# Bias products first, table transfers on SyncE, half of a down product held at the change of phase

## The chip, the cores and the metric

The kernel runs on one core of a Trainium2 chip. The metric is the device time of one launch in microseconds (us); a smaller time is better. The kernel is written in a Python layer in which tiles and instructions are traced in program order. A planner then fixes the order of the instructions on every engine when the program is built, from a simulated timeline (`schedule_with_timeline_sim=True`): of the instructions that are ready in the simulation, the one that stands earlier in the program goes first. On the chip every engine works through its list in that fixed order.

## The reference, cut to what matters

One decoder layer is run for 1024 prompt tokens and 64 sample tokens, in float32, with model width 1024 and inner width 2816:

```python
x = x + 0.5 * swiglu(rmsnorm(x, norm_ffn1), ffn1_w_up, ffn1_w_down)   # FFN 1
h = rmsnorm(x, norm_mix);  q, k, v, u, g_a, g_b = split(h @ w_in)
A = dilated_attention(q, k, v, relative_bias)     # three head groups
B = multiscale_pool(u)
x = x + (sigmoid(g_a) * (A @ w_a) + sigmoid(g_b) * (B @ w_p)) @ w_out
x = x + 0.5 * swiglu(rmsnorm(x, norm_ffn2), ffn2_w_up, ffn2_w_down)   # FFN 2

def swiglu(x, w_up, w_down):
    gate, up = split(x @ w_up)
    return (silu(gate) * up) @ w_down
```

The relative bias is a table of 32 rows (one for each bucket of distance) by 12 heads. It is looked up by distance and added to the logits of the attention. The outputs also hold new key and value caches, which for the most part are copies of the old ones.

## The kernel before, in words

**Products.** Each float32 operand is split into a high and a low part (`split`, L216: ScalarE writes the high part, VectorE or GpSimd subtracts it), and each product is three matmuls (`mm3`, L266): high by high, high by low, low by high.

**The FFN (`ffn`, L411, called once for each FFN).** The product with `w_up` is made in blocks of two by two with seven products instead of eight, in the manner of Strassen and Winograd. The tokens are cut into two phases: phase 0 has 512 tokens (two halves of 256), phase 1 has 576 (two halves of 288). A phase has 11 columns `j` (`jj` counts 22 over both phases), and a column has two units, `kind` 0 for the gate and `kind` 1 for the up part. A unit loads two tiles `ur` of 512 KB (`load_unit`, L418, four buffers, so two units) and makes seven left sides from them (`prepare`, L426: four additions on GpSimd at L435 to L440, and seven splits). The left sides are made `LEAD` = 5 products ahead of the product that uses them (`product`, L449). The first product of a unit is copied out by ScalarE at L526.

The seven right sides of a phase are made once, from the tokens' rows, by `right_sides` (L373): VectorE scales by the row statistics (L382), GpSimd and VectorE subtract (L389), ScalarE and VectorE split (L394, L395). They all lie in `h_hi` and `h_lo`, where the right sides of the phase before also lie.

`result` (L512) turns the products of the two units into the hidden column: VectorE adds (L520), VectorE multiplies by the gate (L522), ScalarE makes the high part `hh` (L217) and GpSimd the low part `hl` (L218). The product with `w_down` of a column (`down`, L471) follows one column later. `down_some` (L486) places two of its eight output blocks `d` at each of four places between the products of the next column. `down_weights` (L460) loads and splits the two halves of a column's `w_down` into tiles `wh` and `wl`, of which there are three sets. At the end of phase 0 all eight blocks of the last column follow together (L543), and then the right sides of phase 1 are made; at the end of phase 1 the last column is done for the tokens in two chunks (L546), and `hook` starts the norm of what follows (L645 in FFN 1) or emits the output transposes (FFN 2).

**The start.** SyncE loads nine tiles of rows (`xn`, L583). TensorE transposes them into `xt` (L596), and ScalarE and VectorE evict (L602, L604). The statistics of the first four tiles are made along the way, and with them the right sides of phase 0 (L617). Then `biases` (L562) makes four products of the one-hot table `oh` with the bias table `tb` (L570), copies them to `fr` (three buffers, L572) and sends them to DRAM as `f_scr` (L573, a GpSimd transfer). The pools of these tiles (`bp` and `ip`) are closed at L619, and `ffn` opens its own pool in the same room.

**The tables.** From `f_scr` 47 transfers between L626 and L639, all issued by GpSimd, spread the bias into tables in DRAM for the attention: 44 pieces of `b_scr` (the smallest 1 KB) and three tables `f_rep` of 896 KB. The first reader of any of them runs after FFN 1.

**Order between jobs.** The `Interleaver` (L74) keeps a clock of its own, in planned microseconds, which `mm3` and `down` advance; a job spawned on it runs its next step when its planned time has come. `some_copies` (L210) places copies of the old caches behind the last weight load on SyncE.

The functions that the change touches:

Of the kernel before, what the change touches and what calls it, by code (L numbers as in the profile page):

```python
# [119 lines left out]
def body(ctx, tc, x_prompt, x_sample, c128, c512, c2048, state_pool, rel_bias_table,  # L120
# [290 lines left out]
    def ffn(xt, gi, w_up, w_down, hook):  # L411


        fctx = ExitStack()
        fp = fctx.enter_context(tc.tile_pool(name="fp", bufs=1, side="right"))
        raws, s1s, left, downs = {}, {}, {}, {}

        def load_unit(n):  # L418
            if n < 44:
                c0 = (n % 2) * DFF + (n % 22 // 2) * 256  # L420
                raws[n] = [fp.tile([P, 4, 256], F32, tag="ur", name="ur", bufs=4) for _ in range(2)]
                for i in range(2):
                    load(raws[n][i], w_up[i * 512:(i + 1) * 512, c0:c0 + 256].rearrange(
                        "(k p) n -> p k n", p=P))

        def prepare(i):  # L426

            n, q = divmod(i, 7)
            if n >= 44:
                return  # L430
            a11, a21 = [raws[n][0][:, :, f * P:(f + 1) * P] for f in range(2)]
            a12, a22 = [raws[n][1][:, :, f * P:(f + 1) * P] for f in range(2)]
            if q == 0:
                s1s[n] = fp.tile([P, 4, P], F32, tag="s1", name="s1", bufs=1)
                G.tensor_tensor(out=s1s[n], in0=a21, in1=a22, op=ALU.add)  # L435
                G.tensor_tensor(out=a21, in0=a11, in1=a21, op=ALU.subtract)
            src = (a11, a12, a11, s1s[n], a21, a22, a12)[q]
            if q == 2:
                G.tensor_tensor(out=a11, in0=s1s[n], in1=a11, op=ALU.subtract)  # L439
                G.tensor_tensor(out=a12, in0=a12, in1=a11, op=ALU.subtract)  # L440
            left[i] = [fp.tile([P, 4, P], F32R, tag=x, name=x, bufs=LEAD + 1) for x in ("sh", "sl")]
            split(*left[i], src)
            if q == 6:
                del raws[n]
                load_unit(n + 2)

        made = [0]

        def product(i, p):  # L449
            while made[0] <= i + LEAD:  # L450
                prepare(made[0])
                made[0] += 1
            lh, ll = left.pop(i)
            bank = psa()[:, :PHASES[p][1]]
            mm3(bank, [(lh[:, k, :], ll[:, k, :], *operand(p, i % 7, k)) for k in range(4)],
                0.36)
            il.advance(0.36)
            return bank

        def down_weights(jj, f):  # L460
            r = wp.tile([P, D], F32, tag="wr", name="wr", bufs=3)
            load(r, w_down[(2 * (jj % 11) + f) * P:(2 * (jj % 11) + f + 1) * P, :])
            w = [wp.tile([P, D], F32R, tag=x, name=x) for x in ("wh", "wl")]
            for a in range(2):
                sl = slice(a * 512, (a + 1) * 512)
                split(w[0][:, sl], w[1][:, sl], r[:, sl], G)
            downs.setdefault(jj, []).append(w)
            if f == 0:
                some_copies(1)

        def down(jj, hid, d, c0, n):  # L471
            hh, hl = hid
            t0 = PHASES[jj // 11][0]
            o = psb()[:, :n]
            sl = slice(d * P, (d + 1) * P)
            mm3(o, [(downs[jj][f][0][:, sl], downs[jj][f][1][:, sl],
                     hh[:, f, c0 - t0:c0 - t0 + n], hl[:, f, c0 - t0:c0 - t0 + n]) for f in range(2)])
            xd = xt[:, d, c0:c0 + n]
            V.scalar_tensor_tensor(out=xd, in0=o, scalar=0.5, in1=xd, op0=ALU.mult, op1=ALU.add)  # L479
            il.advance(0.0026 * n)  # L480

        def chunks(p):
            t0, m = PHASES[p]
            return [(0, 512)] if p == 0 else [(t0, m), (t0 + m, m)]

        def down_some(jj, hid, ds):  # L486
            if hid is not None:
                for d in ds:
                    for c0, n in chunks(jj // 11):
                        down(jj, hid, d, c0, n)  # L490
                    hook(jj, None, d)

        load_unit(0)
        load_unit(1)
        prev = None
        for jj in range(22):
            p, j = divmod(jj, 11)
            t0, m = PHASES[p]
            if j == 0:
                if p:  # L500
                    right_sides(xt, gi, p, [over_rows(diagonal(st, m)) for st in sts])
                prev = None
            if jj == 1:
                sts = [stat() for _ in range(2)]
                for h in range(2):
                    il.spawn(sumsq(xt, PHASES[1][0] + h * PHASES[1][1], PHASES[1][1], sts[h]), 8 * h)
            hid = [fp.tile([P, 2, 576], F32R, tag=x, name=x, bufs=2) for x in ("hh", "hl")]
            sil = {}
            for kind in range(2):
                n = 2 * jj + kind  # L510

                def result(r, s, bank, part, kept):  # L512

                    if kind == 0:
                        t = sil[r, s] = fp.tile([P, 288], F32, tag="si", name="si", bufs=4)[:, :m]
                        V.tensor_tensor(out=t, in0=part, in1=bank, op=ALU.add)  # L516
                        S.activation(t, t, AF.Silu)
                    else:
                        c = tmp()[:, :m] if kept else part
                        V.tensor_tensor(out=c, in0=part, in1=bank, op=ALU.add)  # L520
                        t = sil[r, s]
                        V.tensor_tensor(out=c, in0=c, in1=t, op=ALU.mult)  # L522
                        split(hid[0][:, r, s * m:(s + 1) * m], hid[1][:, r, s * m:(s + 1) * m], c, G)

                a, b = tmp()[:, :m], tmp()[:, :m]
                S.activation(a, product(7 * n, p), AF.Copy)  # L526
                result(0, 0, product(7 * n + 1, p), a, True)
                V.tensor_tensor(out=a, in0=a, in1=product(7 * n + 2, p), op=ALU.add)
                V.tensor_tensor(out=b, in0=a, in1=product(7 * n + 3, p), op=ALU.add)
                down_some(jj - 1, prev, (4 * kind, 4 * kind + 1))  # L530
                o = product(7 * n + 4, p)
                result(1, 1, o, b, True)
                V.tensor_tensor(out=a, in0=a, in1=o, op=ALU.add)
                if kind:
                    down_weights(jj, 0)
                down_some(jj - 1, prev, (4 * kind + 2, 4 * kind + 3))
                if kind:
                    down_weights(jj, 1)
                result(1, 0, product(7 * n + 5, p), a, False)
                result(0, 1, product(7 * n + 6, p), b, False)  # L540
            prev = hid
            if j == 10 and p == 0:
                down_some(jj, prev, range(KD))  # L543
            elif j == 10:
                hook(jj, -1, 0)
                for i, (c0, n) in enumerate(chunks(1)):  # L546
                    for d in range(KD):
                        down(jj, prev, d, c0, n)
                        hook(jj, i, d)
        fctx.close()  # L550
# [29 lines left out]
    for t in range(ntile):  # L580
        rows = P if t < 8 else NS
        xn = ip.tile([P, D], F32, tag="xn", name="xn", bufs=7)
        load(xn[:rows], xp[t * P:(t + 1) * P, :] if t < 8 else xs)  # L583
        xns.append(xn)
    first = []
    for tiles in ((0, 1), (2, 3), (4, 5, 6, 7, 8)):
        for t in tiles:
# [27 lines left out]
        first.append(over_rows(dg))  # L615
        if tiles[0] == 2:
            right_sides(xt, 0, 0, first)  # L617
    biases()
    ictx.close()  # L619
    bctx.close()  # L620

    def fbias(g, off, ap):
        return bass.AP(tensor=f_scr.tensor, offset=f_scr.offset + g * 4 * BL + off, ap=ap)


    for g in range(3):  # L626
        G.dma_start(out=b_scr[g][:, :, P:], in_=neg.unsqueeze(1).to_broadcast([NS, 4, NS]))
        if g == 2:
            G.dma_start(out=b_scr[g][:, :, :P], in_=fbias(g, 127, [[0, NS], [BL, 4], [1, P]]))
        else:  # L630
            for q in range(Q):
                G.dma_start(out=b_scr[g][q::Q, :, :P],
                            in_=fbias(g, 127 - q // DIL[g], [[0, B], [BL, 4], [1, P]]))
        for b in range(B):
            G.dma_start(out=b_scr[g][b * Q:(b + 1) * Q, :, P + b * Q:P + (b + 1) * Q],
                        in_=fbias(g, 384, [[Q, Q], [BL, 4], [1, Q]]))

    for g in (0, 1, 3):
        G.dma_start(out=f_rep[g], in_=fbias(g, 0, [[BL, 4], [0, P], [1, BL]]))  # L639

    def spill(c):
        c0, n = CH[c]
# [794 lines left out]
```

## Time and profile before

| | |
|---|---|
| three runs | 2517.49, 2519.24, 2520.58 us; median 2519.24 us |
| profiled execution | 2517.62 us, span 2515.9 us from first to last instruction |
| TensorE matmul busy | 2363.3 us (94%) |
| VectorE, GpSimd, ScalarE busy | 1817.6 (72%), 1136.1 (45%), 975.9 us (39%) |
| mean granted TensorE clock | 0.953 of full speed |

The rows further down are of one profiled execution. PE is the matmul side of TensorE, DVE is VectorE, ACT is ScalarE, POOL is GpSimd, SP is SyncE, and a trailing q (SPq) is an engine's sequencer, which issues transfers. "L271 psa<-h_hi,sh" names the line, the written tile and the tiles read; lines 271 to 273 are the three matmuls of `mm3`. "[4.58 <-ACT hh L217]" behind an instruction says how long its engine was idle before it and what ended that. A granted clock of 1.00 is 2.4 GHz and 0.50 is 1.2 GHz.

### The profile page before, as it was taken

The numbers are of one execution on the slowest core, as the hardware profiler recorded it, in microseconds if no ns is written. First come the engines' busy times: TensorE is split into PE (matmuls) and PEld (weight loads), VectorE is DVE, ScalarE is ACT, GpSimd is POOL, SyncE is SP. The second block draws the span as 40 slices with busy tenths as digits, with TensorE's granted clock in tenths as the row PEclk, the third lists the DMA queues.
The fourth block names the chain that finished last, engine by engine and source line by source line (L and its number), as shares of the span: only waits on it lengthen the run. The fifth ranks groups of instructions, "written<-read, shape, count | busy, mean of one in ns | idle before, by whom it ended". The sixth has DMA issues, their size and how long they took to land. (4 is left out here: it accounts for less than half of the span.)

```text
span 2515.9 us, 42145 instructions
## 1 busy us (share of the span) xinstructions
PE 2363.3 (94%) x15894; PEld 2235.3 (89%) x15894; DVE 1817.6 (72%) x3246; ACT 975.9 (39%) x2130; POOL 1136.1 (45%) x1060
## 2 busy tenths in 40 slices
PE   4499999799999989999999999997999998999999
PEld 2489998699999989999999889996899987999998
DVE  5498888788888863366677424629988888788886
ACT  4244444343443433344333222214444443444442
POOL 6656666556555431201011110105666665566554
PEclk7799999799999989999899999997999997999999
DMA  6223343333324122457565773622244432333251
GB/s 189 78 80 109 109 134 134 124 101 118 118 101 134 50 68 83 152 163 233 181 193 177 244 233 118 217 76 75 88 140 140 152 138 68 126 127 127 92 201 38
DMA packets 208314, 328.72 MB, mean 131 GB/s; under 512 B 16272, under 2 KB 171600, under 8 KB 207328
## 3 DMA queue, kind: packets, MB, share of 16 engines
q1 hardware_dynamic: 194096, 293.48, 35.6%
q0 software_dynamic: 14016, 32.56, 3.7%
q8 instruction: 125, 2.05, 0.3%
q14 instruction: 77, 0.63, 0.1%
HBM read 297.10 MB, written 76.32 MB: 148 GB/s over the span
## 5 line engine op out<-in xcount | busy, mean ns | idle before, releaser
L271 PE MATMUL psa<-h_hi,sh 128*128 128x256 f32 (+1 forms) x2464 | 724.9, 295 | 62.1 <-ACT sh L217 51.0
L272 PE MATMUL psa<-h_lo,sh 128*128 128x256 f32 (+1 forms) x2464 | 727.9, 295 | 18.7 <-DVE h_lo L395 18.3
L273 PE MATMUL psa<-h_hi,sl 128*128 128x256 f32 (+1 forms) x2464 | 723.1, 294 | 0.0
L218 DVE TENSOR_TENSOR sl<-ur,sh 128x512 fp32r<-128x512 f32 x528 | 589.5, 1123 | 109.9 <-ACT sh L217 99.9
L271 PEld LDWEIGHTS psa<-h_hi,sh 128*128 128x128 f32 x2464 | 474.2, 193 | 77.4 <-ACT sh L217 52.8
L272 PEld LDWEIGHTS psa<-h_lo,sh 128*128 128x128 f32 x2464 | 474.7, 193 | 33.6 <-DVE h_lo L395 29.3
L273 PEld LDWEIGHTS psa<-h_hi,sl 128*128 128x128 f32 x2464 | 475.6, 193 | 0.5 <-DVE sl L218 0.5
L217 ACT ACTIVATE sh<-ur 128x512 fp32r<-128x512 f32 x528 | 330.3, 627 | 370.3 <-POOL ur L439 187.2
L272 PE MATMUL psa<-h_lo,wh 128*128 128x360 f32 (+1 forms) x1104 | 374.7, 339 | 5.5 <-DVE h_lo L364 5.5
L271 PE MATMUL psa<-h_hi,wh 128*128 128x360 f32 (+1 forms) x1104 | 376.6, 342 | 3.4 <-ACT h_hi L363 3.4
L273 PE MATMUL psa<-h_hi,wl 128*128 128x360 f32 (+1 forms) x1104 | 370.9, 336 | 0.0
L272 PE MATMUL psb<-hl,wh 128*128 128x288 f32 (+1 forms) x1056 | 349.0, 331 | 6.2 <-POOL hl L218 6.2
L271 PE MATMUL psb<-hh,wh 128*128 128x288 f32 (+1 forms) x1056 | 338.0, 336 | 13.3 <-ACT hh L217 11.5
L273 PE MATMUL psb<-hh,wl 128*128 128x288 f32 (+1 forms) x1056 | 348.5, 331 | 0.0
L218 POOL TENSOR_TENSOR hl<-tmp,hh 128x288 fp32r<-128x288 f32 (+1 forms) x176 | 171.7, 984 | 378.4 <-ACT hh L217 378.4
L479 DVE SCALAR_TENSOR_TENSOR xt<-psb,xt 128x288 f32<-128x288 f32 (+1 forms) x528 | 260.8, 526 | 76.2 <-PE psb L273 75.3
L218 POOL TENSOR_TENSOR wl<-wr,wh 128x512 fp32r<-128x512 f32 x176 | 259.0, 1492 | 93.5 <-ACT wh L217 49.2
L217 ACT ACTIVATE wh<-wr 128x512 fp32r<-128x512 f32 (+1 forms) x284 | 157.9, 615 | 177.9 <-PE psa L272 112.9
L272 PEld LDWEIGHTS psa<-h_lo,wh 128*128 128x128 f32 x1104 | 214.2, 194 | 10.3 <-DVE h_lo L364 5.8
L271 PEld LDWEIGHTS psa<-h_hi,wh 128*128 128x128 f32 x1104 | 213.6, 194 | 10.6 <-issue 5.0
L271 PEld LDWEIGHTS psb<-hh,wh 128*128 128x128 f32 x1056 | 194.9, 190 | 29.4 <-ACT hh L217 12.4
L272 PEld LDWEIGHTS psb<-hl,wh 128*128 128x128 f32 x1056 | 200.7, 190 | 22.4 <-POOL hl L218 8.6
(262 smaller groups left out, 3416.9 us busy)
## 6 DMA issues: line engine op xcount, KB each, us to landing
ur<-in_ffn_w_up_dram SPq DMA_DIRECT2D x176, 512.0 KB, 3.9
wr<-in_ffn_w_down_dram SPq DMA_DIRECT2D x88, 512.0 KB, 5.7
out_dram<-in_cache_kv_w_dram SPq DMA_DIRECT2D x32, 1020.0 KB, 7.6
qb<-q_scr SPq DMA_DIRECT2D x96, 256.0 KB, 4.4
wr<-in_w_in_dram SPq DMA_DIRECT2D x38, 512.0 KB, 4.7
kt<-in_cache_kv_w_dram SPq DMA_DIRECT2D x64, 256.0 KB, 4.3
vt<-in_cache_kv_w_dram SPq DMA_DIRECT2D x26, 512.0 KB, 7.9
t<-t_scr SPq DMA_DIRECT2D x16, 544.0 KB, 5.0
```

What stands on the lines that cost most here:

```text
L217: S.activation(hi, src, AF.Copy)
L218: eng.tensor_tensor(out=lo, in0=src, in1=hi.bitcast(F32), op=ALU.subtract)
L271: PE.matmul(out, lh, rh, start=i == 0, stop=False)
L272: PE.matmul(out, lh, rl, start=False, stop=False)
L273: PE.matmul(out, ll, rh, start=False, stop=i == n - 1)
L479: V.scalar_tensor_tensor(out=xd, in0=o, scalar=0.5, in1=xd, op0=ALU.mult, op1=ALU.add)
```

## The change

Three edits, in the diff below. `biases()` is called before the transposes instead of behind them. The 47 table transfers are issued by SyncE instead of GpSimd, each behind the last load issued so far, as a job of the interleaver that starts at planned time 60 and gives way for 6 planned us after each small piece and 20 after each `f_rep`. And in the last column of each phase (`j == 10`, `kind` 1) the four blocks of the down product of column 9 are not placed between the seven products but behind them, followed by the second half of the last column's weights; in phase 1 the hook that starts the next norm now stands ahead of these four blocks.

```diff
@@ ffn
-                down_some(jj - 1, prev, (4 * kind, 4 * kind + 1))
+                held = kind and j == 10
+                if not held:
+                    down_some(jj - 1, prev, (4 * kind, 4 * kind + 1))
                 o = product(7 * n + 4, p)
                 result(1, 1, o, b, True)
                 V.tensor_tensor(out=a, in0=a, in1=o, op=ALU.add)
                 if kind:
                     down_weights(jj, 0)
-                down_some(jj - 1, prev, (4 * kind + 2, 4 * kind + 3))
-                if kind:
-                    down_weights(jj, 1)
+                if not held:
+                    down_some(jj - 1, prev, (4 * kind + 2, 4 * kind + 3))
+                    if kind:
+                        down_weights(jj, 1)
                 result(1, 0, product(7 * n + 5, p), a, False)
                 result(0, 1, product(7 * n + 6, p), b, False)
+            if j == 10:
+                if p:
+                    hook(jj, -1, 0)
+                down_some(jj - 1, prev, range(4, KD))
+                down_weights(jj, 1)
             prev = hid
             if j == 10 and p == 0:
                 down_some(jj, prev, range(KD))
             elif j == 10:
-                hook(jj, -1, 0)
@@ start
         xns.append(xn)
+    biases()
     first = []
...
             right_sides(xt, 0, 0, first)
-    biases()
     ictx.close()
     bctx.close()
@@ tables
-    for g in range(3):
-        G.dma_start(out=b_scr[g][:, :, P:], in_=neg.unsqueeze(1).to_broadcast([NS, 4, NS]))
...
-    for g in (0, 1, 3):
-        G.dma_start(out=f_rep[g], in_=fbias(g, 0, [[BL, 4], [0, P], [1, BL]]))
+    def later(out, in_):
+        with tc.issue_after(last_load[0].ins):
+            nc.sync.dma_start(out=out, in_=in_)
+
+    def tables():
+        for g in range(3):
+            later(b_scr[g][:, :, P:], neg.unsqueeze(1).to_broadcast([NS, 4, NS]))
+            yield 6
...
+        for g in (0, 1, 3):
+            later(f_rep[g], fbias(g, 0, [[BL, 4], [0, P], [1, BL]]))
+            yield 20
+
+    il.spawn(tables(), 60)
```

## Rows read from the trace of the kernel before

**Rows 1.** Waits of TensorE, whole span: us in total, times, longest.

```profile
PE psa L271 <- ACT sh L217: 51.0, 2, 35.4
...
PE psb L271 <- ACT hh L217: 11.5, 3, 4.6
```

**Rows 2.** Windows: length, busy us (x count) by engine, granted clock, DMA share, GB/s.

```profile
39.00:54.60 15.60, 0.04 (x1) 0.00 (x0) 4.77 (x12) 3.13 (x8) 15.58 (x27) 0.50 0.41 91
...
60.40:95.80 35.40, 0.01 (x1) 0.00 (x0) 0.86 (x3) 1.93 (x5) 19.36 (x28) 0.55 0.18 53
...
438.00:442.60 4.60, 0.06 (x1) 0.00 (x0) 4.13 (x4) 1.30 (x3) 4.60 (x4) 1.00 0.39 102
...
442.60:446.00 3.40, 1.75 (x5) 0.91 (x5) 0.00 (x0) 0.00 (x0) 3.25 (x4) 0.58 1.22 473
...
446.00:450.00 4.00, 4.00 (x10) 3.13 (x11) 0.69 (x1) 0.00 (x0) 0.00 (x0) 0.50 0.32 131
...
450.60:458.10 7.50, 7.50 (x33) 6.02 (x33) 3.93 (x6) 0.70 (x2) 0.00 (x0) 1.00 0.01 2
...
861.00:866.30 5.30, 3.00 (x13) 2.88 (x13) 4.67 (x10) 1.39 (x3) 2.92 (x3) 0.69 0.25 85
```

**Rows 3.** Timeline of the start: start us, us, engine, line, operation, [idle before].

```profile
29.21 0.69 PE L596 MATMUL psb<-ident,xn 64*128 64x64 f32 x4 [0.47 <-ACT xt L602]
...
45.61 0.52 POOL L573 DMA_DIRECT2D f_scr<-fr  x1
...
48.22 0.94 SPq L191 DMA_DIRECT2D ur<-in_ffn_w_up_dram  x2
```

**Rows 4.** Timeline of GpSimd at 90 us.

```profile
90.03 1.09 POOL L639 DMA_DIRECT2D f_rep<-f_scr  x1 [11.59 <-issue]
...
91.13 1.28 POOL L435 TENSOR_TENSOR s<-ur 128x512 f32<-128x512 f32 x1
```

**Rows 5.** Timeline: from the second row statistic to the second unit, both FFNs.

```profile
18.56 1.26 DVE L382 SCALAR_TENSOR_TENSOR tmp<-xt,gains,psb 128x256 f32<-128x256 f32 x3 [0.34 <-PE psb L351]
...
110.55 0.37 ACT L526 ACTIVATE tmp<-psa 128x256 f32<-128x256 f32 x1
...
1711.37 1.26 DVE L382 SCALAR_TENSOR_TENSOR tmp<-xt,gains,psb 128x256 f32<-128x256 f32 x3
...
1740.96 0.36 ACT L526 ACTIVATE tmp<-psa 128x256 f32<-128x256 f32 x1
```

**Rows 6.** Timeline of VectorE: one eviction, one bias copy, four low parts.

```profile
26.27 0.68 DVE L604 COPY xt<-psb 128x512 f32<-128x512 f32 x1
...
33.64 0.61 DVE L572 COPY fr<-psb 4x448 f32<-4x448 f32 x1
...
97.52 4.66 DVE L218 TENSOR_TENSOR sl<-ur,sh 128x512 fp32r<-128x512 f32 x4
```

**Rows 7.** Groups by line, the bias products: busy us, mean ns, idle before.

```profile
L570 PE MATMUL psb<-oh,tb 33*4 33x448 f32 x8 | 6.3, 936 | 2.9 <-DVE xt L604 2.1 <-DVE fr L572 0.8
```

**Rows 8.** DMA issues: out<-in, queue, count, KB each, median us to landing.

```profile
f_rep<-f_scr POOLq DMA_DIRECT2D x3, 896.0 KB, 12.5
...
out_dram<-in_cache_kv_w_dram SPq DMA_DIRECT2D x32, 1020.0 KB, 7.6
...
b_scr<-f_scr POOLq DMA_DIRECT2D x24, 1.0 KB, 1.9
...
oh<-in_onehots_dram POOLq DMA_DIRECT2D x1, 231.0 KB, 7.5
```

**Rows 9.** Timeline of SyncE and GpSimd in the steady part of the first FFN.

```profile
319.66 0.37 SPq L191 DMA_DIRECT2D ur<-in_ffn_w_up_dram  x1
...
326.47 1.30 POOL L435 TENSOR_TENSOR s<-ur 128x512 f32<-128x512 f32 x1 [2.01 <-DMA ur<-in_ffn_w_up_dram]
```

**Rows 10.** Timeline of GpSimd at the first FFN's change of phase.

```profile
440.14 3.12 POOL L218 TENSOR_TENSOR wl<-wr,wh 128x512 fp32r<-128x512 f32 x2
```

**Rows 11.** Timeline of TensorE behind the first FFN.

```profile
885.12 0.67 PE L272 MATMUL psa<-h_lo,wh 128*128 128x360 f32 x1 [5.46 <-DVE h_lo L364]
```

More of the change, by code (lines that the diff above doesn't have):

```diff
@@ L623, in fbias @@
         return bass.AP(tensor=f_scr.tensor, offset=f_scr.offset + g * 4 * BL + off, ap=ap)
-    for g in range(3):
-        G.dma_start(out=b_scr[g][:, :, P:], in_=neg.unsqueeze(1).to_broadcast([NS, 4, NS]))
[L628 to L636, printed above, removed]
-    for g in (0, 1, 3):
-        G.dma_start(out=f_rep[g], in_=fbias(g, 0, [[BL, 4], [0, P], [1, BL]]))
+    def later(out, in_):
[5 more added lines that the diff above has]
+            yield 6
+            if g == 2:
+                later(b_scr[g][:, :, :P], fbias(g, 127, [[0, NS], [BL, 4], [1, P]]))
+                yield 6
+            else:
+                for q in range(Q):
+                    later(b_scr[g][q::Q, :, :P],
+                          fbias(g, 127 - q // DIL[g], [[0, B], [BL, 4], [1, P]]))
+                    yield 6
+            for b in range(B):
+                later(b_scr[g][b * Q:(b + 1) * Q, :, P + b * Q:P + (b + 1) * Q],
+                      fbias(g, 384, [[Q, Q], [BL, 4], [1, Q]]))
+                yield 6
+        for g in (0, 1, 3):
+            later(f_rep[g], fbias(g, 0, [[BL, 4], [0, P], [1, BL]]))
+            yield 20
+    il.spawn(tables(), 60)
     def spill(c):
```

## The prediction

> **What bounds the kernel now.** I read the page first: TensorE is busy 94% of the span, so a change can win only in its idle time and in its time at half clock. The slices of the span show both in the first two of 40 and around the changes of phase. Next I read TensorE's waits. Two of them alone, for the high part of a left side, are 51.0 us; three for the hidden column's high part are 11.5 us [rows 1]. The windows say where: of 39.0 to 54.6 TensorE works 0.04 us, of 60.4 to 95.8 it works 0.01 us [rows 2], while GpSimd issues transfers. In FFN 1's change of phase it idles 4.54 of 4.60 us and 1.65 of 3.40 us, and then runs 4.00 us at a granted clock of 0.50 [rows 2].
>
> The timeline tells why the two long gaps are there. The last transpose starts at 29.21, but the first load of `ur` is issued only at 48.22, behind the last transfer of `fr`, issued at 45.61 [rows 3]: the room of `ur` was that of `fr`, and this transfer stands on GpSimd among table transfers. The second gap ends when GpSimd has issued the last `f_rep` at 90.03, before which it stood 11.59 us, and can begin the first addition of the left sides at 91.13 [rows 4]. So the start is bound by GpSimd's list, not by any data that TensorE needs from the tables.
>
> **The start.** Bias products first takes the transfer of `fr` out of the way of `ur`; the move to SyncE takes 47 issues, and the waiting before them, from GpSimd. What is late then is VectorE, which makes right sides. FFN 2 has the same start with no table transfers: from the scaling behind its second row statistic at 1711.37 to the end of the first copy of its second unit (1740.96 + 0.36 = 1741.32) are 29.95 us [rows 5]. In FFN 1 the same two points lie at 18.56 and 110.92 [rows 5]. To FFN 2's 29.95 us I add what VectorE there had behind it: five evictions of transposes at 0.68 (3.4), four bias copies at 0.61 (2.4), and the low parts of six left sides at 4.66 / 4 = 1.17 (7.0) [rows 6], together 12.8. The bias products take 6.3 us of TensorE [rows 7]; now they stand ahead of the transposes and wait for `oh`, which took 7.5 us to land [rows 8]. They can push the statistics back by nothing (TensorE has idle time there) up to 6.3; I take half, 3.2. Their four transfers to DRAM stay on GpSimd, at 0.52 each [rows 3]; they come earlier, ahead of the right sides' subtractions, and I cost these 2.1 us at nothing, as VectorE is the later of the two engines there; uncovered they would cost 2.1. So the second unit's first copy ends at 18.56 + 29.95 + 12.8 + 3.2 = 64.5, and the gain is 110.92 - 64.5 = 46.4. Upper bound: both gaps wholly, 15.56 + 35.39 = 51.0 [rows 2]. Lower bound: the load comes at 29.9 + 6.3 = 36.2, 12.0 before 48.22, the second gap goes, and VectorE's 12.8 are wholly exposed: 12.0 + 35.4 - 12.8 = 34.6.
>
> **The tables on SyncE.** The job starts at planned time 60, so the first weights are past. Each of 44 small pieces lands in some 1.9 us, an `f_rep` in 12.5 [rows 8]. A weight load has little slack: one issued at 319.66 was waited for by GpSimd until 326.47, 2.01 us of it idle [rows 9], with a cache copy of 7.6 us [rows 8] on the same queue; no wait of TensorE stands beside it, as left sides are made five products ahead. An `f_rep` in the copy's place is 12.5 - 7.6 = 4.9 longer. Three of them cost between nothing and 14.7; I take 2, near nothing, since the copies, the nearest row in kind, cost nothing. The small pieces I cost at nothing: their cover is the same lead, and without it each would cost its 1.9.
>
> `f_rep` as a transfer is written by four outer rows. The Trainium skill, DMA: Bandwidth & Descriptors, section "Why a DMA increments its semaphore by 16 and not by 1", says that a transfer uses only as many DMA engines, up to 16, as divide its outermost dimension, so `f_rep` would use four. The trace agrees: 896 KB in 12.5 us beside 1020 KB in 7.6 [rows 8]. Its section on queues gives SyncE one ring on each engine, so that loads behind would wait on those four. By the copies' row the three tables cost next to nothing; by that rule the lead may be too short, which is a rival below.
>
> **Held blocks, change of phase.** Now TensorE has nothing between the last product and the hidden column. 32 matmuls of a down block take 7.50 us at full clock [rows 2], 0.234 each, six to a block, so 1.4 a block and 5.6 for the four held. The chain from the last product (438.06) to the last low part (just before 446.0) is 7.9 us, and 3.12 of it are the second half of the weights, which GpSimd splits ahead of the hidden column [rows 10]. That half now stands behind the held blocks, so the chain is 4.8, under 5.6: the idle 4.54 + 1.65 = 6.2 goes. So does the half clock: 4.00 us at 0.50 [rows 2] lose 2.0. Together 8.2. New is a wait: the second weight half needs a set that the held blocks free, so its 3.12 on GpSimd come after them, and the right sides' first work is queued behind on GpSimd and ScalarE. The first half's matmuls of four blocks, 4 x 3 x 0.234 = 2.8, cover most of it. I charge 1.5; bounds are nothing and 3.1 with 2.0 of half clock. So 6.7 (3.1 to 8.2). FFN 2 repeats it: its wait is one of the three in 11.5 [rows 1]. Two changes: 13.4.
>
> **Ends of the FFNs.** Behind FFN 1's last product TensorE idles 5.30 - 3.00 = 2.30 us, and 3.00 us at 0.69 lose 0.9 [rows 2]. Held blocks cover this, and the norm starts earlier; I take 3.0. Nothing is the lower bound; with the norm's own stall of 5.46 [rows 11] it is 8.7 at most. FFN 2's end has no such wait: nothing to gain, and the late weights can cost up to 3.1; I take 0.5.
>
> **Sum.** 46.4 + 13.4 + 3.0 - 0.5 - 2.0 = 60.3. The profiled execution took 2517.62 us (span 2515.9), so 2457.3; the median of the runs is 1.62 above it, which gives 2459. With all bounds together it is 2443 to 2496.
>
> **The rivals.**
> - The bias products hold TensorE until `oh` lands, and transposes, statistics and VectorE's extra work come late. For it: `oh` landed late [rows 8]. Against: TensorE was half idle among the transposes. The start then gives its lower bound, 34.6: 2471.
> - The bias edit doesn't do what it says: the first `ur` still waits, for another tile in its room, and the first gap stays. Against: the transposes' own tiles are free by 30 [rows 3]. 15.6 less: 2474.
> - The held blocks give nothing: the wait for the second weight half takes the place of the wait for the hidden column. For it: GpSimd's 3.12 [rows 10]. 13.4 and 3.0 less: 2475.
> - Three `f_rep` on four rings each hold the weights for all of 12.5 us [rows 8]. 37.5 instead of 2: 2494. The Trainium skill's page named above bears on this one.
> - The other side: the 47 transfers make SyncE's queue the bound. Each holds the weight loads for its whole landing: 44 x 1.9 + 3 x 12.5 = 121 [rows 8], which gives 2459 - 2 + 121 = 2578. It decides from the point where more than 62 us of these 121 reach TensorE. For it: the load that was already 2.01 late [rows 9]. Against: a small piece is 1.9 against a copy's 7.6, and the copies reach TensorE nowhere in the steady part.
>
> **How the numbers follow.** The forecast (2459, its own range 2450 to 2468) has 0.63; late bias products 0.13, the first gap staying 0.07, held blocks without gain 0.08, long `f_rep` 0.05, SyncE's queue 0.04. The range 2445 to 2480 takes in the first four and leaves out the last two and a little of the tails. A measurement of this kernel can tell 0.2%, or 5.0 us, from no change. All cases but the last are faster by more than that; of the last a quarter might end about even. So faster 0.96, same 0.01, slower 0.03.
>
> **What would show it.** Right: the first `ur` is issued near 30 to 36 instead of 48; GpSimd's first addition follows the landing; the second unit's first copy ends near 64; the waits for the left side's high part shrink from 51.0 to a few us, and waits for low parts of right sides appear instead. At both changes of phase the wait for `hh` is gone and the granted clock is 1.00 until the right sides begin. Wrong: SyncE's weight loads land late around the three `f_rep`, and GpSimd's first addition waits for a DMA with TensorE idle behind it; or TensorE waits for `wl` after the held blocks; or the statistics come after 25 us.

## The result and the profile after

The changed kernel takes 2457.26 us, median of 3 runs (2455.30 to 2461.50), against 2519.24 before: ratio 0.9758, 95% interval 0.9735 to 0.978. The profiled execution is the run of 2457.26 us, with a span of 2455.4. The forecast was 2459. The total is right, but its terms are not: the start gave 34 us and not 46, and some 11 us that I had not forecast came from the end of FFN 1 to the start of FFN 2. The experiments were made to find out which part of the change gave what.

First the busy times of the page, then TensorE's waits in the changed kernel (us in total, times, longest). They answer to [rows 1]. Lines behind 550 have moved: L577 is the bias product, L579 its copy to `fr`, L604 the transposes, L634 the table transfers.

```profile
PE 2356.4 (96%) x15894; PEld 2227.4 (91%) x15894; DVE 1806.4 (74%) x3246; ACT 974.0 (40%) x2130; POOL 1107.7 (45%) x1013
```

```profile
PE psb L577 <- DVE ist L301: 14.6, 1, 14.6
...
PE psb L604 <- DVE fr L579: 7.3, 1, 7.3
PE psa L271 <- ACT sh L217: 4.9, 1, 4.9
...
PE psb L271 <- ACT hh L217: 2.2, 2, 1.1
```

The 51.0 us for a left side have become 4.9, and the 11.5 for the hidden column 2.2. But two new waits stand in the start, 14.6 and 7.3 us, both on the bias products' side. The timeline shows how they hang together, of TensorE, VectorE, GpSimd, SyncE and ScalarE in turn (start, duration, what was done, idle before):

```profile
14.60 6.13 PE L577 MATMUL psb<-oh,tb 33*4 33x448 f32 x8 [14.60 <-DVE ist L301]
...
30.75 1.12 PE L604 MATMUL psb<-ident,xn 128*128 128x128 f32 x4 [7.28 <-DVE fr L579]
...
45.83 0.69 PE L604 MATMUL psb<-ident,xn 64*128 64x64 f32 x4 [0.47 <-ACT xt L610]
51.45 0.58 PE L271 MATMUL psa<-h_hi,sh 128*128 128x256 f32 x1 [4.93 <-ACT sh L217]
...
30.09 0.61 DVE L579 COPY fr<-psb 4x448 f32<-4x448 f32 x1 [10.21 <-DMA f_scr<-fr]
...
36.36 1.25 DVE L382 SCALAR_TENSOR_TENSOR tmp<-xt,gains,psb 128x256 f32<-128x256 f32 x3
...
18.34 7.39 POOL L218 TENSOR_TENSOR wl<-wr,wh 128x512 fp32r<-128x512 f32 x6 [11.48 <-ACT wh L217]
25.68 1.55 POOL L580 DMA_DIRECT2D f_scr<-fr  x3
...
46.55 3.03 SPq L191 DMA_DIRECT2D ur<-in_ffn_w_up_dram  x4
...
76.06 0.37 ACT L526 ACTIVATE tmp<-psa 128x256 f32<-128x256 f32 x1
```

All eight bias products stand first on TensorE. They begin at 14.60; `oh`, issued at 6.3 and landed 8.2 us later, is just there (the wait is written to VectorE, whose `ist` came last by the profile; in the run with the norm's start in its old place the same wait is written to `oh`'s transfer, 15.1 us). So no tile is transposed before 20.7, where the kernel before had its second row statistic ready at 18.56 [rows 5]. Then VectorE stands 10.21 us at the fourth copy to `fr`: there are three rooms, and GpSimd issues the first transfer out of one only at 25.68, behind six low parts of weights (18.34, 7.39 us). TensorE waits 7.28 us behind it for a PSUM bank. The scaling behind the second row statistic begins at 36.36, 17.8 us after that of before [rows 5]; the last transpose begins at 45.83 and the first `ur` is issued behind it at 46.55, only 1.67 before the 48.22 of [rows 3]. The second gap is gone: the second unit's first copy begins at 76.06 (before 110.55 [rows 5]).

At FFN 1's change of phase the windows (columns as in [rows 2]) answer to its rows of 438 to 450. The held blocks fill 398.30 to 404.10 at full clock; behind them TensorE idles 1.12 us for `hh`, and GpSimd's second half of the weights comes after:

```profile
398.30:404.10 5.80, 5.78 (x26) 4.33 (x24) 5.80 (x9) 1.24 (x3) 4.13 (x3) 1.00 0.27 86
```

```profile
405.20 1.25 PE L271 MATMUL psb<-hh,wh 128*128 128x512 f32 x3 [1.12 <-ACT hh L217]
...
405.94 5.05 POOL L218 TENSOR_TENSOR wl<-wr,wh 128x512 fp32r<-128x512 f32 x4
```

The end of FFN 1, in windows that cover nearly the same work, first before and then after (the second has 7 matmuls more and ends 1.2 us later in the work). TensorE's idle time is 11.6 and 10.0 us; what differs more is the granted clock, 0.78 and 0.93. It loses 11.9 and 3.4 us over these windows, and 9.0 and 2.2 of them while TensorE was busy:

```profile
858.00:912.00 54.00, 42.36 (x224) 40.39 (x223) 46.66 (x111) 20.23 (x43) 21.91 (x43) 0.78 0.28 96
```

```profile
817.00:865.00 48.00, 37.97 (x231) 34.85 (x230) 40.87 (x109) 19.83 (x44) 17.48 (x40) 0.93 0.32 109
```

To see where time was won I compare the start of ScalarE's copy of each unit's first product (L526, 88 of them) and, between the FFNs, the same matmul of the two kernels. The table gives gains in us against the first profile of before, for five of the kernels and for a second execution of before: the first and the last column the gain so far, those between what each stage added.

| kernel | start (unit 5) | rest of phase 0 (to 21) | change of phase | end of FFN 1 | to FFN 2 | rest of phase 0 | change of phase | end (unit 87) |
|---|---|---|---|---|---|---|---|---|
| changed | 32.6 | +1.6 | +6.8 | +7.2 | +6.5 | -1.4 | +8.1 | 60.9 |
| bias products first alone | -5.2 | +1.6 | +0.3 | +1.2 | -5.8 | 0.0 | +0.8 | -7.2 |
| tables alone | 40.2 | +1.6 | -0.1 | +0.3 | +7.9 | +0.2 | +1.0 | 51.2 |
| held blocks alone | -0.1 | +1.6 | +6.8 | +7.2 | +0.5 | 0.0 | +8.1 | 24.2 |
| tables and held blocks | 41.6 | +0.3 | +6.7 | +6.1 | +9.9 | 0.0 | +8.1 | 73.0 |
| before once more | -1.7 | +0.3 | -0.1 | +0.5 | +1.4 | 0.0 | +0.8 | 1.2 |

"Start" is unit 5, where the kernels have settled; "end of FFN 1" is from unit 43 to the 25th matmul with `h_lo` behind it. Units 22 to 43 and 66 to 87 have no column: they add at most 0.7 either way. The last row tells how much two executions of one kernel differ. The +1.6 in "rest of phase 0" also stands where the edit changed nothing there (held blocks alone), so it is no part's gain.

### The profile page after: what moved, and what is told of

The parts are those of the page before. It is cut to its first block, busy times and chain, and to the rows that moved or that the text cites. A ratio compares the mean times of both kernels' runs of the same rounds, so it can differ in the third digit from the quotient of the medians.

```text
span 2455.4 us, 42164 instructions
## 1 busy us (share of the span) xinstructions
PE 2356.4 (96%) x15894; PEld 2227.4 (91%) x15894; DVE 1806.4 (74%) x3246; ACT 974.0 (40%) x2130; POOL 1107.7 (45%) x1013
## 4 chain that ended last, share of the span: by engine, by line
PE 44%; DVE 4%; issue 1%; DMA 1%; POOL 1%; ACT 0%; SPq 0%; DVEq 0%; POOLq 0%; ACTq 0%
PE psa L272 10%; PE psa L271 10%; PE psa L273 10%; PE psb L271 4%; PE psb L272 3%; PE psb L273 3%; DVE h_lo L395 1%; DMA rt<-u_scr 1%; PE psb L1205 1%; DVE sl L218 1%; DMA qb<-q_scr 1%; PE psb L1019 0%; DVE tmp L382 0%; PE psb L1398 0%; PE psb L984 0%
## 5 line engine op out<-in xcount | busy, mean ns | idle before, releaser
L272 PE MATMUL psa<-h_lo,sh 128*128 128x256 f32 (+1 forms) x2464 | 729.1, 296 | 19.1 <-DVE h_lo L395 18.6
L273 PEld LDWEIGHTS psa<-h_hi,wl 128*128 128x128 f32 x1104 | 211.8, 192 | 4.4 <-issue 3.5
```

The costliest lines, as they stand in the source:

```text
L272: PE.matmul(out, lh, rl, start=False, stop=False)
L273: PE.matmul(out, ll, rh, start=False, stop=i == n - 1)
```

## The experiments

Each ran beside the kernel before on the same chip; ratios are against it. "Changed kernel" is the one with all three parts.

**One part at a time.** The first kernel is before with the call of `biases()` moved, the second before with the tables' job, the third before with the held blocks and the earlier norm.

```
         xns.append(xn)
+    biases()
     first = []
...
-    biases()
     ictx.close()
```

> Only the bias products are put ahead of the transposes; the table transfers stay on GpSimd, the down products are not held. Theory (the second gap of the start is made by GpSimd's table transfers, the first by the transfer of fr): the first load of ur is issued near 46.6 as in the changed kernel, the first product starts some 5 us earlier or not at all, and the second gap stays, since GpSimd still issues 47 transfers ahead of the left sides: gain 0 to 10 us. Rival (the bias products first are what opens the start, and the tables are issued by GpSimd while it has nothing else to do): the second gap shrinks as well, gain 25 to 35 us.

It is slower: 2529.03 us against 2519.09, ratio 1.0038 (1.0024 to 1.0052). Theory's mechanism is right and its sign too kind: by the table's row 5.2 us are lost in the start, and 5.8 in the stage to FFN 2, to which I come below. GpSimd issues 44 of the 47 transfers from 32.46 on and stands before the last two `f_rep`, and now the right sides are queued behind them there: VectorE waits 16.38 and 10.66 us for GpSimd's part of a right side, TensorE 17.19 and 12.04 behind it.

```profile
74.61 1.11 POOL L639 DMA_DIRECT2D f_rep<-f_scr  x1 [11.60 <-issue]
86.85 1.09 POOL L639 DMA_DIRECT2D f_rep<-f_scr  x1 [9.71 <-issue]
```

```profile
76.50 0.48 DVE L382 SCALAR_TENSOR_TENSOR tmp<-xt,gains,psb 128x256 f32<-128x256 f32 x1 [16.38 <-POOL h_lo L395]
...
90.62 0.48 DVE L382 SCALAR_TENSOR_TENSOR tmp<-xt,gains,psb 128x256 f32<-128x256 f32 x1 [10.66 <-POOL tmp L389]
```

The tables alone:

```
-        G.dma_start(out=b_scr[g][:, :, P:], in_=neg...)
+            later(b_scr[g][:, :, P:], neg...)
+            yield 6
...
+    il.spawn(tables(), 60)
```

> Only the table transfers go to SyncE; the bias products stay behind the right sides, the down products are not held. Theory (the second gap is GpSimd's table transfers): the first gap stays, 15.6 us of it, the second gap of 35.4 goes but for the copies and additions that stood beside it: gain 25 to 35 us, nearly all that the changed kernel gains in its start (34.5). If so, the bias products first were worth under 5 us, because their own 14.6 us of waiting for oh cost the right sides what they gave ur. Rival (both gaps need both edits): gain under 15 us, and the sum with the run before gives the 34.5 only together.

2470.96 us, ratio 0.9804 (0.9791 to 0.9818). The start gains 40.2, more than in the changed kernel, so the rival falls; the theory has the right gap, but its 25 to 35 us were too few. The second gap is gone. The first stayed for the most part: TensorE stands 12.15 us before its first product, where before it stood 15.58. With the products behind the transposes, as before the change, `ur` is issued at 44.42: 3.8 us earlier than before (48.22), since GpSimd issues `fr`'s transfers without table transfers between them, and 2.1 us earlier than in the changed kernel (46.55).

```profile
44.42 0.94 SPq L191 DMA_DIRECT2D ur<-in_ffn_w_up_dram  x2
...
51.53 0.58 PE L271 MATMUL psa<-h_hi,sh 128*128 128x256 f32 x1 [12.15 <-ACT sh L217]
```

The held blocks alone:

```
+                held = kind and j == 10
+                if not held:
+                    down_some(jj - 1, prev, (4 * kind, 4 * kind + 1))
...
+            if j == 10:
+                if p:
+                    hook(jj, -1, 0)
+                down_some(jj - 1, prev, range(4, KD))
+                down_weights(jj, 1)
```

> Only the four down blocks are held at the two changes of phase and at the ends of the FFNs, with the norm started ahead of them; start and tables as before. Theory A (the gains of 6.8 and 8.1 us at the two changes of phase and 7.4 at the end of FFN 1 are the held blocks' own; the further 6.3 us between there and FFN 2 come of another order of the planner and of the clock, and don't belong to them): gain 20 to 23 us. Theory B (the earlier norm also saves the 6.3 us in the attention): gain 27 to 30 us. Rival (part of it comes of GpSimd's and SyncE's changed lists): under 15 us.

2497.54 us, ratio 0.9916 (0.9901 to 0.993), a gain of 21.6, inside theory A's 20 to 23; theory B is too large. The three places give 6.8, 7.2 and 8.1 us, as in the changed kernel to the tenth.

By the medians the three gains are -9.9, 48.1 and 21.6, together 59.8; the changed kernel gained 62.0 and, in a second measurement below, 59.9. The parts add up, and one of them is a loss.

**The wait for `fr`.** Four rooms in place of three:

```
-            fr = bp.tile([4, BL], F32, tag="fr", name="fr", bufs=3)
+            fr = bp.tile([4, BL], F32, tag="fr", name="fr", bufs=4)
```

> The changed kernel with four rooms for fr instead of three. Theory (VectorE stands 10.2 us for the first transfer of fr, which GpSimd issues only behind six low parts of weights, and TensorE waits 7.3 us behind it for psb; all of it delays the right sides): VectorE's wait and TensorE's 7.3 go, the right sides start 6 to 8 us before 36.4, the first load of ur comes 4 to 8 us earlier, and the time falls by 4 to 8 us against the changed kernel, to 2449 to 2453. Rival (ur's room is freed by the last transfer of fr or by the transposes' tiles, so the load is bound by GpSimd's list and not by VectorE): the right sides start earlier but the first ur stays within 2 us of 46.6: 2455 to 2458.

2453.71 us, ratio 0.9736 (0.9721 to 0.9751). VectorE's 10.21 us and TensorE's 7.28 are gone (the wait for `oh` stays), the scaling behind the second row statistic starts at 28.57 in place of 36.36, `ur` is issued at 40.31, 6.2 us earlier, and the start gains 39.1, 6.5 more. The theory holds, though the time is 0.7 above its range; the rival doesn't.

```profile
40.31 0.95 SPq L191 DMA_DIRECT2D ur<-in_ffn_w_up_dram  x2
```

**Without the bias products first.** The changed kernel with `biases()` back behind the right sides (the first diff reversed):

> The changed kernel with the bias products back behind the right sides: tables on SyncE and held blocks stay. Theory (the bias products first cost the start more than they give: alone they made the second unit's first copy 3.9 us later, and with the tables alone on SyncE it came 40.9 us earlier, against 34.5 in the changed kernel): the second unit's first copy near 69.7 as with the tables alone, and the time 4 to 9 us under the changed kernel's: 2448 to 2453. Rival (the bias products first are needed for what stands behind the start, since SyncE's first table transfer waits for f_scr ahead of ur): within 3 us of the changed kernel, 2454 to 2460.

2448.82 us, ratio 0.9728 (0.9715 to 0.9741), a gain of 69.95 where the tables and the held blocks alone gave 48.1 + 21.6 = 69.7. The theory holds. This kernel beats the changed one: its five runs, 2445.17 to 2452.51 us, lie below all eight of that one, 2453.65 to 2461.50. From four rooms for `fr` (2446.65 to 2454.53) the runs don't set it apart. Its profiled execution was the shortest of its five runs (2445.17), so its column "to FFN 2" in the table is rather high.

**Between the tiles.** The products behind the first two tiles' statistic, and four rooms:

```
-    biases()
...
         first.append(over_rows(dg))
+        if tiles[0] == 0:
+            biases()
         if tiles[0] == 2:
             right_sides(xt, 0, 0, first)
```

> The changed kernel with the bias products behind the first two tiles' row statistic instead of ahead of all tiles, and four rooms for fr. Theory (two things hold the first load of ur: the end of the last transpose, and the last transfer of fr; ahead of the tiles the products delay the one by their wait for oh, behind them they delay the other, and between the tiles neither is late): the last transpose ends near 33 to 36, the first ur is issued within 1 us of it, the first product starts near 39 to 43 (51.5 in the changed kernel), and the time is 6 to 12 us under the changed kernel's: 2445 to 2451. Rival (then VectorE, which makes the right sides and evicts the transposes, is the later one whatever the place of the bias products): the second unit's first copy stays near 69 as with the tables alone or with four rooms for fr, 2449 to 2454.

`ur` is issued at 36.65, ten us earlier than in the changed kernel, and the first product starts at 41.85, as the theory said. It hardly helps: unit 0's copy starts at 52.48, against 53.55 where `ur` came at 43.73, and unit 5 gains 42.1, against 41.6. VectorE is busy 10.65 of the 10.65 us behind the start of the first product, so the rival is right that VectorE is the later one there:

```profile
41.85:52.50 10.65, 8.36 (x28) 6.60 (x28) 10.65 (x16) 6.07 (x16) 9.03 (x9) 0.50 0.32 105
```

The time, 2459.15 (0.9763, 0.975 to 0.9776), is outside what either expected; the attention stretch, to which I come below, took 319.8 us in its profile.

**The norm's start.** One line back to its old place, the blocks held as changed:

```
             if j == 10:
-                if p:
-                    hook(jj, -1, 0)
                 down_some(jj - 1, prev, range(4, KD))
...
             elif j == 10:
+                hook(jj, -1, 0)
```

> The changed kernel with the last norm's start back behind the held blocks (one line moved), which are held as in the changed kernel. Theory (at the end of FFN 1 the held blocks cover the wait for the hidden column and its half clock, 3.2 us by the windows of before, and the other 4 of the 7.2 us gained there come of the earlier norm): the first matmul behind the norm comes 3 to 5 us later than in the changed kernel, the time 2458 to 2463. Rival (the 7.2 are the held blocks' alone, the norm's start is hidden): within 2 us of the changed kernel there.

The end of FFN 1 gains 1.9 us, where with the earlier norm it gains 7.2 in the changed kernel (3.9 to 7.2 over the eight profiles that have it). So the held blocks are at most 1.9, of which kernels without the edit show 0.3 to 1.2 there, and the earlier norm is 4.0 against the second execution of the changed kernel and 5.3 against the first, about as the theory had it. The norm's stall shows in the waits from 819 to 873, where the changed kernel has 1.1 us for this line:

```profile
PE psa L272 <- DVE h_lo L364: 6.8, 2, 6.1
```

The time, 2474.37 (0.9822, 0.9808 to 0.9835), is 11 above the range: the stage to FFN 2 adds -6.0 here, where it adds 6.5 in the changed kernel (the attention stretch took 323.3 us).

**All tables in one row.** The job's pauses set to nothing:

```
-            yield 6
+            yield 0
...
-            yield 20
+            yield 0
```

> The changed kernel with SyncE's 47 table transfers issued in one row instead of one every 6 to 20 us of planned time. Theory (SyncE goes on to the next transfer when it has issued one, some 0.6 us each, and does not wait for its landing): one load of weights stands behind about 30 us of issues once, the left sides made ahead and the loads two units ahead cover most of it, and the time is 0 to 12 us above the changed kernel's, 2457 to 2469. Rival (a transfer holds the queue for all of its landing, 44 x 1.9 + 3 x 12.5 = 121 us by the rows of before; spread over 250 us this was hidden): TensorE stalls for 60 to 100 us behind it, 2520 to 2560.

2481.67 us, ratio 0.9854 (0.9841 to 0.9867): 24 above the changed kernel, between the two. SyncE issues the 47 from 131.90 to 171.56, 39.7 us, and does not wait for each one's landing; TensorE then waits 19.13 us for the left sides. Of 121 us of landings no more than these 40 stood in the queue, but the lead covers only some 13 of them: 26.4 us are gone at unit 12.

```profile
131.48 0.37 SPq L191 DMA_DIRECT2D ur<-in_ffn_w_up_dram  x1
...
143.86 11.01 SPq L634 DMA_DIRECT2D b_scr<-f_scr  x16
...
156.15 0.63 SPq L634 DMA_DIRECT2D f_rep<-f_scr  x1
157.01 11.97 SPq L634 DMA_DIRECT2D b_scr<-f_scr  x8
169.03 2.53 SPq L634 DMA_DIRECT2D f_rep<-f_scr  x2
171.67 16.72 SPq L191 DMA_DIRECT2D ur<-in_ffn_w_up_dram  x4
```

```profile
192.44 0.58 PE L271 MATMUL psa<-h_hi,sh 128*128 128x256 f32 x1 [19.13 <-ACT sh L217]
```

**VectorE relieved.** Tables and held blocks, with `fr` copied by ScalarE and four rooms for it:

```
-            V.tensor_copy(fr, o)
+            S.activation(fr, o, AF.Copy)
```

> Tables on SyncE, held blocks, bias products behind the right sides as before the change; the copies of fr go from VectorE to ScalarE, with four rooms for fr. Theory (VectorE is the late engine of the start: its fourth copy of fr came only at 40.9 us and held the first ur to 43.7): the first ur is issued 2 to 4 us earlier, VectorE loses 2.4 us of copies, the second unit's first copy comes 2 to 4 us before 68.4, and the time is 1 to 5 us under the run with VectorE's copies: 2444 to 2448. Rival (the right sides' own work holds the units behind, as with the bias products between the tiles, where ur came 7 us earlier and only 0.5 us was left at the fifth unit): unit 5 within 1 us, the time within 3 us of 2448.8.

`ur` is issued at 41.55 in place of 43.73 and the second unit's copy starts 2.1 us earlier (66.34), but unit 5 gains 42.3 against 41.6. The rival is right about the start; the time, 2456.63 (0.9754, 0.9741 to 0.9768), is above what both said. The attention stretch took 317.7 us.

**The same kernels again.** No edit.

> The changed kernel once more, unaltered, for a second profiled execution. Theory (of the 13.7 us gained between the ends of FFN 1 and the start of FFN 2, 7.2 are the end of FFN 1 and the other 6.5 are the attention stretch, whose length differs from execution to execution; four rooms for fr left TensorE's order as it was and still had 314.8 us for the stretch that took 307.1): the start, the changes of phase and FFN 1's end are the same within 1 us, the attention stretch is anywhere from 305 to 323 us, and if it is over 311 the step is shown. Rival (the stretch is set by the order in which the instructions stand): 307 within 1.5 us.

> The kernel before once more, unaltered, for a second profiled execution. By the theory that the attention stretch varies from execution to execution, it is anywhere from 305 to 323 us and everything ahead of it the same within 1 us; by the rival, 317.5 within 1.5 us.

The changed kernel: 2458.55 us, ratio 0.9758 (0.9745 to 0.9771), like the first time. Before: one run of 2516.46. The attention stretch is cut from the 289th to the 673rd matmul of a high left with a low right side between the FFNs; these windows are of before, before again, changed, changed again, four rooms for `fr`, and tables with held blocks:

```profile
1070.08:1387.60 317.52, 309.96 (x2032) 295.22 (x2031) 216.61 (x468) 122.39 (x372) 38.46 (x68) 0.95 0.61 190
```

```profile
1071.03:1388.14 317.11, 307.21 (x2032) 291.85 (x2031) 216.08 (x468) 122.61 (x372) 38.51 (x68) 0.96 0.61 191
```

```profile
1023.20:1330.29 307.09, 305.32 (x2032) 292.09 (x2031) 217.75 (x468) 122.11 (x372) 38.46 (x68) 0.96 0.63 197
```

```profile
1023.87:1334.22 310.35, 307.41 (x2031) 293.80 (x2031) 218.21 (x469) 122.06 (x372) 38.48 (x68) 0.96 0.62 195
```

```profile
1018.01:1332.85 314.84, 307.93 (x2033) 293.82 (x2032) 217.62 (x468) 122.14 (x372) 38.43 (x68) 0.96 0.60 192
```

```profile
1013.03:1319.44 306.41, 302.96 (x2033) 289.03 (x2031) 217.38 (x468) 121.99 (x372) 38.56 (x68) 0.97 0.63 197
```

The work is the same (counts of all engines); TensorE's idle time goes from 1.8 to 9.9 us, and the granted clock from 0.95 to 0.97. For the changed kernel neither expectation is met: its second execution is 3.3 us off its first, more than the rival's 1.5, and with 310.4 it is under the 311 that I had set as the proof. For before the second execution, 317.1, is where the rival had it, and its start is 1.7 us later than the first's, more than the 1 us that I had allowed. The changed kernel's start is 33.1, its changes of phase 6.8 and 8.0, as the first time within 0.5; the end of FFN 1 gave 5.9 and not 7.2.

## Why the prediction was right, and where it was wrong

**The start: the step failed, and a rival names the first cause.** I took 46.4; it gave 34.5 at the second unit and 32.5 to 34.2 behind it in phase 0. The step that failed is "They can push the statistics back by nothing ... up to 6.3; I take half, 3.2". The right sides were pushed back by 17.8 us: by the wait for `oh`, by the products' own 6.13, and by VectorE's 10.21 at `fr`, of which [rows 8] (7.5 to land) and [rows 3] (GpSimd's late issue) already showed the makings. I had counted what the products take of TensorE and not what stands behind them in its order. The rival "bias products hold TensorE until `oh` lands" names the first cause. That its 34.6 for the start is what came is chance: it was made of a load of `ur` at 36.2, which came at 46.55, and of 12.8 us of VectorE. The wait for a room of `fr` was in no case of mine. By my own mark (wrong if "the statistics come after 25 us") the step was wrong. Of the signs of being right, the waits for a left side's high part did shrink to 4.9 us, but the first `ur` did not come near 30 to 36, and TensorE's waits for low parts of right sides are 18.6 us, where they were 18.3.

**What the start's gain is from.** "Bias products first takes the transfer of `fr` out of the way of `ur`" was wrong too. `ur` waits for the later of the last transpose and `fr`'s last transfer, and first place for the products trades one for the other. The tables on SyncE give the start its 40 us; the products first take back 8 in company (41.6 against 33.8 at unit 20), 8 to 10 by the medians, and alone 9.9 by the medians, 5.2 of it in the start. Without that delay my terms, 18.56 + 29.95 + 12.8, would end the second copy at 61.3; with that edit undone it began at 68.39 and 69.67, and at 66.3 at the best, behind a stretch that VectorE filled. So some 5 us of my 46.4 were VectorE's work undersized, by that window and not by an experiment of its own.

**Tables on SyncE: right, 0 where I took 2.** TensorE is busy 20.00 us of each 20.00 from 300 to 380, beside the small pieces. One of these went early, at 29.98 and ahead of the first `ur`; the others are issued from 131.19 to 391.81. The three `f_rep` are issued at 445.99, 470.90 and 486.15, and the gain is 41.0 at units 22 and 24. In the changed kernel's profile:

```profile
340.00:360.00 20.00, 20.00 (x149) 18.91 (x148) 17.46 (x26) 9.32 (x20) 15.63 (x12) 1.00 0.52 173
```

```profile
470.90 0.65 SPq L634 DMA_DIRECT2D f_rep<-f_scr  x1
```

The rival in which SyncE's queue is the bound rested on a queue that is held for each landing; the run with all tables in one row shows issue time as the price, some 0.65 us for most of the 47. Behind the first `f_rep` it is more: eight small transfers took 11.97 us there, where sixteen took 11.01 ahead of it. (My 1.9 us for each of 44 landings was that of the smallest; the three pieces of 64 KB took 6.3.) But that run also shows that the spread is what makes the tables free: without it they cost 26 us of the start. That an `f_rep` uses few DMA engines shows in the window in which one runs almost alone: a share of 0.27 of the 16 is busy, as much as 4.3 of them.

```profile
473.45:482.81 9.36, 8.59 (x65) 8.36 (x64) 7.76 (x16) 2.55 (x6) 3.87 (x3) 1.00 0.27 101
```

The Trainium skill, DMA: Bandwidth & Descriptors, section "Why a DMA increments its semaphore by 16 and not by 1", would put it on four engines; the trace agrees, by these 4.3 more than by the 12.5 us beside 7.6 of my prediction.

**Held blocks at the changes of phase: right.** 6.8 and 8.1 us where I took 6.7 each. In FFN 1 the step held as written, but for one term: the chain from the last product to `hh` is still 1.12 us longer than the held blocks, and the late second half of the weights, for which I charged 1.5, shows in no wait of TensorE. In FFN 2 some 0.8 of the 8.1 are not the edit's: runs without it, the repeat of before among them, show 0.8 to 1.0 there.

**End of FFN 1: mis-sized.** 3.0 were taken; 7.2 came, and 3.9 to 7.2 over the kernels that have it. The held blocks' own part is at most 1.9 (I had 3.2). The earlier norm is the larger part, 4.0 to 5.3, and I had put the norm's 5.46 of stall [rows 11] only into the upper bound. The end of FFN 2 was right: 60.9 at the last unit, 60.5 at the end of the span, -0.4 against -0.5.

**To FFN 2: nothing was forecast, 6.5 came.** The attention stretch is 307.1 and 310.4 us in the changed kernel, 317.5 and 317.1 before, so the gain is there in both executions of each. It is not any one part's: with the products first alone the stretch is 323.2, with the tables alone 308.5, with the held blocks alone 316.2. What sorts the 13 profiles is the order that the planner chose. GpSimd's instructions stand there in one of two orders. The six profiles with the changed kernel's order (changed twice, tables alone, four rooms for `fr`, tables with held blocks, all tables in one row) take 306.4 to 314.8 us; the seven with before's order (before twice, products first alone, held blocks alone, products between the tiles, the norm's old start, `fr` by ScalarE) take 316.2 to 323.3. So three kernels with the tables on SyncE got the longer stretch (products between the tiles, the norm's old start, `fr` by ScalarE), and the times of these three came out above the ranges set for them. That it is GpSimd's order that does it is not shown: the other engines' orders differ too.

The order is not all. Kernels with one and the same order on every engine (changed twice, four rooms, all tables in one row) take 307.1, 310.4, 314.8 and 306.5. Four of the five runs with four rooms lie between 2453.64 and 2454.53 us and the fifth at 2446.65, a step of about this size. What differs is TensorE's idle time, 1.8 to 12.7 us over the 13 profiles, and what the clock loses (the length times what is missing to 1.00), 8.5 to 18.8; without these two the stretch is 293 to 296 us in every profile. Which wait starts the one or the other course I have not settled.

So the total of 60.3 against 60.5 by the spans is luck, two errors that cancel: 12 us too much for the start, and 4 too little for the end of FFN 1, 6.5 for the attention, 2 for the tables and 1.4 for the second change of phase; the other -2 are spread over the units.

## What to carry to other kernels

A product moved ahead on an in-order engine brings its own wait along: price the landing of its operand, and the room of its result as well as its duration. Transfers that nothing needs soon belong on a queue that has slack, and spread out; in a row the same 47 cost 26 us. And try each part of a change alone: here one of three was a loss of 8 to 10 us inside a gain of 60, and leaving it out is the better kernel (2448.82).

## What the runs showed of the hardware that I had not expected

TensorE can fall to its lower clock (granted 0.50, 1.2 of 2.4 GHz) while it is busy all the time. In the attention there are rows of 34 or 36 matmuls of two columns each, and in such a row or right behind it the clock falls although TensorE does not idle; in the kernel before, in the one that starts at 1254.06:

```profile
1254.06 6.10 PE L865 MATMUL psb<-halves,sqs 128*128 128x2 f32 x36
```

```profile
1252.00:1256.00 4.00, 4.00 (x35) 4.00 (x34) 3.67 (x6) 0.38 (x1) 0.54 (x1) 0.94 0.81 268
1256.00:1264.00 8.00, 8.00 (x38) 7.97 (x38) 1.69 (x8) 1.26 (x4) 0.00 (x0) 0.50 0.76 252
```

All 18 such rows of three kernels (before, changed, four rooms) have a stretch at 0.50 in them or right behind them, with TensorE busy all of it. It is not without exception: with tables and held blocks one of the six, at 923.28, keeps the full clock:

```profile
923.28:931.28 8.00, 8.00 (x63) 7.92 (x62) 7.83 (x21) 1.58 (x4) 1.07 (x2) 1.00 0.18 70
```

GpSimd stands at its issue of a large transfer behind many others (11.60 and 9.71 us before an `f_rep` in the run with the bias products first, 11.59 in [rows 4]); SyncE's issue of the same three took 0.60 to 0.69 us each when spread out.
